# The order of high and low products in sixteen experts of a hybrid diffusion step

## The chip, the cores and the metric

The kernel runs on one core of a Trainium2 chip. The metric is device time in microseconds (us) of one execution. Lower is better. The engines are named as the profile names them: PE is TensorE (matmuls), PEld its weight loads, DVE is VectorE, ACT is ScalarE, POOL is GpSimd, SP is SyncE, which issues the loads of weights.

## The reference, cut to what matters

The program is one layer of a hybrid backbone: a token mixer, and then a mixture of experts in which every expert picks its own tokens. The change lies in the experts alone.

```python
# bsz 1; 16 experts; d 1024; f 2048; 128 latent tokens and 16 prompt tokens for each expert
hid = jax.nn.silu(jnp.einsum('becd,edf->becf', xs, w1)) * jnp.einsum('becd,edf->becf', xs, w3)
out = jnp.einsum('becf,efd->becd', hid, w2) * gate[..., None]
```

Weights and activations are fp32.

## The kernel before, in words

**Parts.** An fp32 weight chunk (`raw`, 512 rows by 512 columns, 1 MB) is split into a high part `hi` in fp32r (a cast on ACT, L1294) and a low part `lo` in bf16, which is the rest (a subtraction on DVE, L1300). The tokens `x2` hold their own high and low part side by side in 288 columns, `xb` the tokens in bf16 in 144 columns. A product needs both: a high matmul `hi` times 288 columns (L1485), and a low matmul `lo` times 144 columns (L1493), which adds to the second half of the same accumulator. `sums` then adds the two halves: a copy on ACT (L1498) and an add on DVE (L1499).

**An expert's first product** (w1 and w3). Four steps `fb`, in each the two weights `w`, and for each of these two chunks (the two halves of the 1024 rows) and two blocks `q` of 256 columns. A block is 16 high matmuls, then 16 low ones, then its `sums`. So an expert has 16 blocks.

**Its second product** (w2). Two halves `dh` of the output, in each four chunks `kq` and two accumulators `q`. For every chunk: 8 high and 8 low matmuls of `q` 0, 8 high and 8 low ones of `q` 1. `sums` stand behind the fourth chunk. The second half of the last expert is ordered in another way, two chunks at a time for each `q`.

**What sets the order.** The program is written out by hand: each engine runs its instructions in the order of the code, and waits on semaphores. `ahead(n)` issues the splits of the chunks before `n`, five chunks in front of the products (`AH` is 5), with the low part one chunk behind the high part:

```python
def sums(a, dst):
    b = ep.tile([P, 2, S], F32, name="bs", bufs=3)
    A.copy(b, a[:, :, S:2 * S])
    V.tensor_tensor(dst, a[:, :, :S], b, op=OP.add)
```

There are six buffers of `hi` and of `lo`, five of `raw`, and three accumulators `ac` (`acc_pair`, two PSUM banks each). When a low part is made, the load of the chunk five on is issued by SP (L1288).

**Small groups between the products.** Eight matmuls that make the next expert's list of tokens (`list_make`, L1168), eight transposes of its tokens (`to_cols`, L1424), and eight of the expert before for its result (`finish`, L1509) stand between two blocks. In the first expert a search for thresholds runs beside the products: `step` sends a group of eight small matmuls (L1394) behind a block's high matmuls, and each needs the `msk` (L1387) that DVE made of the one before. Its end leads to the list of the second expert and the gather of that expert's tokens (`xg`, L1335). In the last expert the half result is added into memory and read back (`last_half`, L1571) while the second half runs, and `last_add` (L1552) needs it.

Of the kernel before, what the change touches and what calls it, by code (L numbers as in the profile page):

```python
# [19 lines left out]
P = 128  # L20
# [16 lines left out]
KF = FF // P  # L37
CAP = 128
PCAP = 16
S = CAP + PCAP  # L40
# [9 lines left out]
def hybrid_step_kernel(ctx: ExitStack, tc: tile.TileContext, x_prompt, x_sample, state_lru, c, c_ctx,  # L50
# [4 lines left out]
    V, A, G, PE, SY = nc.vector, nc.scalar, nc.gpsimd, nc.tensor, nc.sync  # L55
# [179 lines left out]
    first = {"v": 512, "p": 0, "g1": 1536, "g2": 2560, "bp": 0, "bl": 0}  # L235
    need = []
    for i, (kind, j) in enumerate(seq):
        if kind == "m":
            q, h = divmod(j, 2)
            need.append((i, wm[h * 512:(h + 1) * 512, 2048 + q * 256:2048 + (q + 1) * 256], 4, 256))  # L240
        elif kind == "a":
            g, h = divmod(j, 4)
            need.append((i, wm[2 * h * P:2 * (h + 1) * P, :2 * D].rearrange("(k p) (z f) -> p k z f", p=P, z=2)
                         [:, :, :, g * 256:(g + 1) * 256], 2, 512))
        else:
            w = w_br_pool[0] if kind == "bp" else w_br_lru[0] if kind == "bl" else w_in[0]
            c0 = first[kind] + j * P
# [200 lines left out]
    for q in range(4):  # L448
        k = 2 * q
# [296 lines left out]
    while at[0] + 1 < len(seq):  # L746
        at[0] += 1
        i = at[0]
        kind, j = seq[i]
# [15 lines left out]
        w = spl.pop((kind, j))  # L765
        if kind == "bp":
            a3 = dense(w, KP, pool_sb["yh"], pool_sb["yl"], KP - 1 if j == 0 else 0)
        elif kind == "bl":
# [4 lines left out]
            for n, (y, ws) in enumerate(parts[::-1] if j == KD - 1 else parts):  # L773
                for ch in range(NCH):
                    cs = slice(ch * CH, (ch + 1) * CH)
                    for k in range(KD):
                        for w in ws:
                            PE.matmul(a3[:, ch, :CH], w[:, k, :], y[:, k, cs], start=n == 0 and k == 0 and w is hi,  # L778
                                      stop=n == 1 and k == KD - 1 and w is ws[-1])
# [73 lines left out]
    def row(r):  # L853
        return bass.AP(tensor=rows_d.tensor, offset=rows_d.offset + r * D, ap=[[0, P], [1, D]])
# [371 lines left out]
    n = 4  # L1226
    for i in [1, 0] + list(range(2, NT - 1)):
        n = max(n + 1, 2 * i + 2)
        a, b = (4, KD - 1)
# [52 lines left out]
    SKIP = ((0, 0, 0), (1, 0, 0), (2, 0, 0))  # L1282
    raw, hl, x3s = {}, {}, {}
# [41 lines left out]
    def ahead(n, lag=1):  # L1325
        while nxt[0] < min(n, NC + 1):
            split_hi(nxt[0])
            nxt[0] += 1
            while nxt[1] < nxt[0] - lag:
                split_lo(nxt[1])  # L1330
                nxt[1] += 1
# [143 lines left out]

    yps = {}

    def products(ws, x2, xb, first, last, step=None):


        for r in range(2):
            for a, w, c0, k0 in ws:
                for k in range(4):
                    kk = k0 + k
                    PE.matmul(a[:, r, :2 * S], w[0][:, k, c0 + r * P:c0 + (r + 1) * P], x2(kk), start=kk == first,  # L1485
                              stop=False)
            if step is not None:
                step(r)
        for r in range(2):
            for a, w, c0, k0 in ws:  # L1490
                for k in range(4):
                    kk = k0 + k
                    PE.matmul(a[:, r, S:2 * S], w[1][:, k, c0 + r * P:c0 + (r + 1) * P], xb(kk), start=False,  # L1493
                              stop=kk == last)

    def sums(a, dst):
        b = ep.tile([P, 2, S], F32, name="bs", bufs=3)
        A.copy(b, a[:, :, S:2 * S])  # L1498
        V.tensor_tensor(dst, a[:, :, :S], b, op=OP.add)  # L1499

    def acc_pair():
        return acc3.tile([P, 2, 512], F32, name="ac")
# [14 lines left out]
    last = {}  # L1517
# [87 lines left out]
    find = search()  # L1605
# [18 lines left out]
    base = 0  # L1624
    prev = None
    for e in range(E):
        x2, xb = X.pop(e)
        hh, hb = [], []
        if 0 < e < E - 1:
            hot = list_hot(ep, V, e + 1, slo[:, :, e + 1])  # L1630
        for fb in range(4):
            hs = []
            for w in range(2):
                h = ep.tile([P, 4, S], F32, name=f"h{w}")
                for q in range(2):
                    a = acc_pair()
                    products([(a, hl[base + i], q * 256, 4 * i) for i in range(2)], lambda k: x2[:, k, :],
                             lambda k: xb[:, k, :], 0, 7,
                             (lambda r: None if r == 0 else next(find, None)) if e == 0 and (fb, w, q) not in SKIP else None)
                    sums(a, h[:, 2 * q:2 * q + 2])  # L1640
                    if (e, fb, w, q) == (0, 3, 1, 0):
                        for _ in find:
                            pass
                        hot = list_hot(ep, V, 1, slo[:, :, 1])
                    if (w, q) != (1, 1):
                        ahead(base + q + 1 + AH)
                for i in range(2):
                    del hl[base + i]
                base += 2
                hs.append(h)  # L1650
                if w == 0:
                    A.activation(h, h, AF.Silu)
                if (e, fb, w) == (0, 0, 1):
                    A.dma_start(g2r, row(6))
                    prompt_gate()
                if fb == 1 and w == 0 and 0 < e < E - 1:
                    list_make(ep, e + 1, hot)
                    fetched = x_fetch(hn_d[:, :], lgi[:, e + 1:e + 2])
                if prev is not None and fb == 0 and w == 0:
                    finish(*prev)  # L1660
                    prev = None
                    if e == 8:
                        fp = finish_prompt(0)
                        next(fp)
                if e == 8 and (fb, w) in ((2, 0), (2, 1)):
                    next(fp, None)
                if e == 7 and (fb, w) == (2, 0):
                    pgr = x_fetch(hp_d[:, :], pgi[:, 1:2], "rows")
                if e == 7 and (fb, w) == (3, 1):
                    prompt_cols(1, pgr)  # L1670
            h1, h3 = hs
            hf = ep.tile([P, 4, 2 * S], F32R, name=f"hh{fb}")
            hg = ep.tile([P, 4, S], BF16, name=f"hb{fb}")
            ht = ep.tile([P, 4, S], F32, name="ht")
            V.tensor_tensor(ht, h1, h3, op=OP.mult)
            ahead(base + AH)
            A.copy(hf[:, :, :S], ht)
            A.copy(hg, ht)
            V.tensor_tensor(hf[:, :, S:], ht, hf[:, :, :S].bitcast(F32), op=OP.subtract)
            hh.append(hf)  # L1680
            hb.append(hg)
        ot = ep.tile([P, KD, S], F32, name="ot")
        if e % 8 == 0:
            yps[e // 8] = ep.tile([P, KD, P], F32, name="yps")
        quarter = None
        if e == E - 1:
            last_hot()
            A.activation(ready[:, 0:1], ready[:, 1:2], AF.Sqrt)
        hc, bc = lambda k: hh[k // 4][:, k % 4, :], lambda k: hb[k // 4][:, k % 4, :]
        aa = {}  # L1690
        for dh in range(2):
            for kq in range(4):
                n = 4 * dh + kq
                step = None if quarter is None else lambda r: next(quarter, None)
                if (e, dh) == (E - 1, 1):

                    q, i = divmod(kq, 2)
                    if i == 0:
                        aa[q] = acc_pair()
                    products([(aa[q], hl[base + j], q * 256, 4 * j) for j in (2 * i, 2 * i + 1)], hc, bc, 0, KF - 1, step)  # L1700
                    if i == 1:
                        sums(aa[q], ot[:, 4 + 2 * q:6 + 2 * q])
                else:
                    for q in range(2):
                        if kq == 0:
                            aa[q] = acc_pair()
                        products([(aa[q], hl[base + kq], q * 256, 4 * kq)], hc, bc, 0, KF - 1, step)
                        if kq == 3:
                            sums(aa[q], ot[:, 4 * dh + 2 * q:4 * dh + 2 * q + 2])
                ahead(base + kq + 1 + AH)  # L1710
                if (e, n) == (E - 1, 3):
                    last_half(ot)
                    fp = finish_prompt(1)
                    next(fp)
                    quarter = last_sums(ot)
                if (e, n) == (E - 1, 4):
                    x3s["fg"] = ew.tile([P, 8, 256], F32, name="raw", bufs=RB).rearrange("p a b -> p (a b)")[:, :D]
                    A.dma_start(x3s["fg"], bass.AP(tensor=final_g.tensor, offset=final_g.offset, ap=[[0, P], [1, D]]))
                if e == 0 and n == LM:
                    list_make(ep, 1, hot)  # L1720
                    fetched = x_fetch(hn_d[:, :], lgi[:, 1:2])
                if e + 1 < E and n == (XC if e == 0 else 1):
                    xf = x_cols(e + 1, fetched)
                if e + 1 < E and n == (XP if e == 0 else 3):
                    X[e + 1] = x_parts(xf)
            for i in range(4):
                del hl[base + i]
            base += 4
        q = (e % 8) * PCAP
        G.tensor_tensor(yps[e // 8][:, :, q:q + PCAP], ot[:, :, CAP:],  # L1730
                        modc[:, 2, 0, 8:, None].to_broadcast([P, KD, PCAP]), op=OP.mult)
        prev = (e, ot)
# [84 lines left out]
```

## Time and profile before

| | |
|---|---|
| median of 3 runs | 2134.88 us (2134.04 to 2135.07) |
| the profiled execution, its own time | 2133.28 us |
| its span (first to last instruction) | 2131.5 us |
| mean granted TensorE clock | 0.986 of full speed |
| busy share of the span: PE, PEld, DVE, ACT, POOL | 96%, 92%, 80%, 64%, 10% |
| experts' products | from about 812 us to the end |

The span and the profiled execution's own time belong together; the median is of other executions. A share of busy time is a mean over the program's stages. The granted clock is what the throttle gave to TensorE, as a share of full speed.

In the rows below, a row of a view by stage has the stretch (us from the span's start), its length, each engine's busy time with its count of instructions (PE, PEld, DVE, ACT, POOL), the granted clock, the mean busy share of the 16 DMA engines, and GB/s. A row in order of time has the start, the length, the engine, the line, the operation, what it writes from what, its shape and its count, and in brackets how long its engine sat idle before it and who ended that. Equal instructions that follow each other are one row. Matmuls are pipelined and their ends are modelled, so the time that a run of them takes is read from its start to the start of the next row. The names leave out numbers: `x` is `x2`, `ac` any accumulator. A row of waits has the total in us, how often, and the longest.

### The profile page before, as it was taken

What the parts mean: (1) busy time and instruction counts of PE and PEld (TensorE: products, weight loads), DVE (VectorE), ACT (ScalarE), POOL (GpSimd) and SP (SyncE); (2) the same over time, 40 slices, a digit from 0 to 9 for tenths busy, and PEclk for the clock granted to TensorE, in tenths of its full rate; (3) what the DMA queues carried; (4) which work ended last, traced back from release to release, by engine and by line L of the source; (5) the groups of instructions that cost most, each with busy time, mean ns of one, the idle gap of its engine ahead of it and who ended that gap; (6) DMA issues with size and microseconds to landing.
All of it is one profiled execution on the core that took longest, in us unless ns stands there. A gap on an engine that the chain in (4) does not pass through costs nothing.

```text
span 2131.5 us, 40527 instructions
## 1 busy us (share of the span) xinstructions
PE 2056.4 (96%) x17269; PEld 1962.2 (92%) x17269; DVE 1703.2 (80%) x1833; ACT 1359.8 (64%) x1442; POOL 208.9 (10%) x338
## 2 busy tenths in 40 slices
PE   7999999999999997899999999999999999999995
PEld 4899999999998876899999999999999999999994
DVE  7788987732336378988998998898998898898896
ACT  7577675321113236677877877777777777787783
POOL 0000001010102120010010010011011011001021
PEclk9999999999999999999999999999999999999997
DMA  8134434164654257799999999999999999999995
GB/s 268 58 117 130 128 96 130 56 220 118 205 169 164 109 178 280 278 320 329 343 334 329 336 339 325 342 346 322 329 341 327 334 344 327 334 337 333 334 312 183
DMA packets 304819, 543.91 MB, mean 255 GB/s; under 512 B 16299, under 2 KB 85627, under 8 KB 304638
## 3 DMA queue, kind: packets, MB, share of 16 engines
q1 hardware_dynamic: 285306, 478.56, 64.8%
q0 software_dynamic: 15728, 52.77, 8.5%
q10 hardware_dynamic: 3604, 9.98, 1.3%
q8 instruction: 135, 2.21, 0.4%
q14 instruction: 46, 0.38, 0.1%
HBM read 500.60 MB, written 40.67 MB: 254 GB/s over the span
## 4 chain that ended last, share of the span: by engine, by line
PE 88%; DVE 7%; ACT 2%; DMA 2%; issue 1%; SPq 0%; DVEq 0%; ACTq 0%; POOLq 0%
PE ac L1485 37%; PE ac L1493 17%; PE a L196 6%; PE a L197 6%; PE a L195 6%; PE a L778 5%; DVE lo L1300 2%; PE a L1004 2%; PE a L1006 2%; PE a L1005 2%; DMA xg<-hn_d,lgi 1%; PE tp L1042 1%; PE tp L667 1%; PE tp L1424 1%; PE tp L1509 1%
## 5 line engine op out<-in xcount | busy, mean ns | idle before, releaser
L1300 DVE TENSOR_TENSOR lo<-raw,hi 128x2048 bf16<-128x2048 f32 x384 | 871.2, 2282 | 0.0
L1294 ACT CAST hi<-raw 128x2048 fp32r<-128x2048 f32 x384 | 729.2, 1912 | 4.4 <-DMA raw<-in_exp_w_dram 2.4
L1485 PE MATMUL ac<-x,hi 128*128 128x288 f32 x4096 | 606.2, 300 | 0.0
L1485 PEld LDWEIGHTS ac<-x,hi 128*128 128x128 f32 x4096 | 553.0, 189 | 1.0 <-issue 0.9
L1493 PEld LDWEIGHTS <-lo 128*128 128x128 bf16 x6144 | 379.4, 98 | 36.1 <-DVE lo L1300 0.2
L1485 PE MATMUL ac<-hh,hi 128*128 128x288 f32 x2048 | 332.9, 304 | 0.0
L1498 ACT COPY bs<-ac 128x288 f32<-128x288 f32 x320 | 128.0, 400 | 288.0 <-PE ac L1493 287.7
L1493 PE MATMUL ac<-xb,lo 128*128 128x144 bf16 x4096 | 301.2, 227 | 0.0
L1485 PEld LDWEIGHTS ac<-hh,hi 128*128 128x128 f32 x2048 | 280.0, 189 | 0.0
L197 PE MATMUL a<-hn_hi,lo 128*128 128x384 f32 x624 | 209.8, 336 | 1.6 <-DVE lo L186 1.6
L195 PE MATMUL a<-hn_hi,hi 128*128 128x384 f32 x624 | 209.7, 336 | 0.0
L196 PE MATMUL a<-hn_lo,hi 128*128 128x384 f32 x624 | 209.6, 336 | 0.0
L1493 PE MATMUL ac<-hb,lo 128*128 128x144 bf16 x2048 | 171.8, 227 | 0.0
L1499 DVE TENSOR_TENSOR h<-ac,bs 128x288 f32<-128x288 f32 x256 | 116.0, 453 | 40.6 <-ACT bs L1498 40.2
L186 DVE TENSOR_TENSOR lo<-raw,hi 128x1024 fp32r<-128x1024 f32 (+1 forms) x77 | 88.3, 1165 | 64.4 <-ACT hi L185 64.4
L197 PEld LDWEIGHTS a<-hn_hi,lo 128*128 128x128 f32 x624 | 117.3, 188 | 2.0 <-DVE lo L186 2.0
L195 PEld LDWEIGHTS a<-hn_hi,hi 128*128 128x128 f32 x624 | 117.3, 188 | 0.4
L196 PEld LDWEIGHTS a<-hn_lo,hi 128*128 128x128 f32 x624 | 117.4, 188 | 0.0
L1730 POOL TENSOR_TENSOR yps<-ot,modc 128x128 f32<-128x128 f32 x16 | 36.0, 2247 | 734.6 <-DVE ot L1499 734.6
L185 ACT CAST hi<-raw 128x1024 fp32r<-128x1024 f32 (+1 forms) x77 | 75.9, 1003 | 45.7 <-PE a L196 36.2
L1499 DVE TENSOR_TENSOR ot<-ac,bs 128x288 f32<-128x288 f32 x64 | 29.3, 458 | 69.5 <-ACT bs L1498 69.5
L1335 POOL DMA_INDIRECT xg<-hn_d,lgi x16 | 45.0, 2813 | 258.4 <-ACT bs L1498 138.2
(443 smaller groups left out, 2602.5 us busy)
## 6 DMA issues: line engine op xcount, KB each, us to landing
raw<-in_exp_w_dram SPq DMA_DIRECT2D x380, 1024.0 KB, 7.2
raw<-in_w_in_dram SPq DMA_DIRECT2D x28, 512.0 KB, 4.7
raw<-in_w_mod_dram SPq DMA_DIRECT2D x28, 512.0 KB, 5.4
araw<-in_w_mod_dram SPq DMA_DIRECT2D x18, 256.0 KB, 4.4
g_d<-sg ACTq DMA_DIRECT2D x8, 576.0 KB, 3.2
yh_d<-yh POOLq DMA_DIRECT2D x8, 576.0 KB, 3.2
yl_d<-yl POOLq DMA_DIRECT2D x8, 576.0 KB, 4.6
m_d<-sg POOLq DMA_DIRECT2D x8, 576.0 KB, 4.2
```

The lines of the kernel that those rows point to most:

```text
L185: A.copy(h, raw)
L186: V.tensor_tensor(l, raw, h.bitcast(F32), op=OP.subtract)
L195: PE.matmul(out, whi, xhi, start=first, stop=False)
L196: PE.matmul(out, whi, xlo, start=False, stop=False)
L197: PE.matmul(out, wlo, xhi, start=False, stop=last)
L778: PE.matmul(a3[:, ch, :CH], w[:, k, :], y[:, k, cs], start=n == 0 and k == 0 and w is hi, stop=n == 1 and k == KD - 1 and w is ws[-1])
L1294: A.copy(hl[n][0], raw[n])
L1300: V.tensor_tensor(lo, r, hi.bitcast(F32), op=OP.subtract)
L1485: PE.matmul(a[:, r, :2 * S], w[0][:, k, c0 + r * P:c0 + (r + 1) * P], x2(kk), start=kk == first, stop=False)
L1493: PE.matmul(a[:, r, S:2 * S], w[1][:, k, c0 + r * P:c0 + (r + 1) * P], xb(kk), start=False, stop=kk == last)
L1498: A.copy(b, a[:, :, S:2 * S])
L1499: V.tensor_tensor(dst, a[:, :, :S], b, op=OP.add)
```

## The change

`products` is cut in two functions. `highs` sends the high matmuls of a block, or only its first one in each bank (`part` true), or all but these (`part` false); `lows` sends the low ones. In the first product the two blocks of a pair of chunks are sent as: all highs of block 0, the first highs of block 1 (they clear its accumulator), the lows of block 0, the lows of block 1, the other highs of block 1. The next pair starts with highs. The second product follows the table `PLAN` over its four chunks, where "H", "h" and "L" are highs, first highs, and lows. `sums` of a block stand where its last matmul is now sent, and the splits, loads and small groups stay at their places between the blocks.

```diff
-    def products(ws, x2, xb, first, last, step=None):
+    def highs(ws, x2, first, last, step=None, part=None):
         for r in range(2):
             for a, w, c0, k0 in ws:
                 for k in range(4):
                     kk = k0 + k
-                    PE.matmul(a[:, r, :2 * S], w[0][:, k, c0 + r * P:c0 + (r + 1) * P], x2(kk), start=kk == first,
-                              stop=False)
+                    if part is None or part == (kk == first):
+                        PE.matmul(a[:, r, :2 * S], w[0][:, k, c0 + r * P:c0 + (r + 1) * P], x2(kk), start=kk == first,
+                                  stop=kk == last)
             if step is not None:
                 step(r)
+
+    def lows(ws, xb, last):
         for r in range(2):
...
+    PLAN = (("H", 0), ("h", 1), ("L", 0), ("L", 1), ("H", 1)), (("H", 1), ("H", 0), ("L", 0), ("L", 1)), \
+        (("L", 1), ("L", 0), ("H", 0), ("H", 1)), (("H", 0), ("L", 0), ("L", 1), ("H", 1))
...
+                pairs = [None, None]
                 for q in range(2):
-                    a = acc_pair()
-                    products([(a, hl[base + i], q * 256, 4 * i) for i in range(2)], lambda k: x2[:, k, :],
-                             lambda k: xb[:, k, :], 0, 7,
-                             (lambda r: None if r == 0 else next(find, None)) if e == 0 and (fb, w, q) not in SKIP else None)
+                    step = (lambda r: None if r == 0 else next(find, None)) if e == 0 and (fb, w, q) not in SKIP else None
+                    for n in range(q, 2 - q):
+                        a = acc_pair()
+                        pairs[n] = [(a, hl[base + i], n * 256, 4 * i) for i in range(2)]
+                        highs(pairs[n], lambda k: x2[:, k, :], 0, None, None if n else step, True if n else None)
+                    lows(pairs[q], lambda k: xb[:, k, :], None if q else 7)
+                    if q:
+                        highs(pairs[q], lambda k: x2[:, k, :], 0, 7, step, False)
+                    a = pairs[q][0][0]
                     sums(a, h[:, 2 * q:2 * q + 2])
...
-                    products([(aa[q], hl[base + j], q * 256, 4 * j) for j in (2 * i, 2 * i + 1)], hc, bc, 0, KF - 1, step)
+                    ws = [(aa[q], hl[base + j], q * 256, 4 * j) for j in (2 * i, 2 * i + 1)]
+                    if i == 0:
+                        highs(ws, hc, 0, None, step)
+                        lows(ws, bc, None)
+                    else:
+                        lows(ws, bc, None)
+                        highs(ws, hc, None, KF - 1, step)
...
-                    for q in range(2):
-                        if kq == 0:
+                    left = [q for _, q in PLAN[kq]]
+                    for part, q in PLAN[kq]:
+                        left.remove(q)
+                        if kq == 0 and q not in aa:
                             aa[q] = acc_pair()
-                        products([(aa[q], hl[base + kq], q * 256, 4 * kq)], hc, bc, 0, KF - 1, step)
-                        if kq == 3:
-                            sums(aa[q], ot[:, 4 * dh + 2 * q:4 * dh + 2 * q + 2])
+                        end = KF - 1 if q not in left else None
+                        ws = [(aa[q], hl[base + kq], q * 256, 4 * kq)]
+                        if part == "L":
+                            lows(ws, bc, end)
+                        else:
+                            early = kq == 0 and q == 1
+                            highs(ws, hc, 0, end, None, (part == "h") if early else None)
+                        if end and kq == 3:
+                            sums(aa.pop(q), ot[:, 4 * dh + 2 * q:4 * dh + 2 * q + 2])
```

In the program as built, PE's order in a pair of blocks of the sixth expert's first product was this (`ac_12705` and `ac_12747` are the accumulators of blocks 0 and 1, `hi_12503` and `lo_12504` the parts of the pair's first chunk; rows that only go on with the same are left out):

```order
L1485 MATMUL ac_12705<-x2_12344,hi_12503 128x288 x4
L1485 MATMUL ac_12705<-x2_12344,hi_12549 128x288 x4
...
L1493 LDWEIGHTS lo_12504
L1493 MATMUL ac_12705<-xb_12345,lo_12504 128x144
...
L1485 MATMUL ac_12747<-x2_12344,hi_12503 128x288 x4
...
L1493 MATMUL ac_12747<-xb_12345,lo_12504 128x144
...
L1485 MATMUL ac_12807<-x2_12344,hi_12591 128x288 x4
```

At the same place PE's order is now this (block 1 has the accumulator `ac_12722`, and `ac_12807` is block 0 of the next pair):

```order
L1486 MATMUL ac_12705<-x2_12344,hi_12503 128x288 x4
...
L1486 MATMUL ac_12722<-x2_12344,hi_12503 128x288 x2
L1496 LDWEIGHTS lo_12504
L1496 MATMUL ac_12705<-xb_12345,lo_12504 128x144
...
L1496 MATMUL ac_12722<-xb_12345,lo_12504 128x144
...
L1486 MATMUL ac_12722<-x2_12344,hi_12503 128x288 x3
...
L1486 MATMUL ac_12807<-x2_12344,hi_12591 128x288 x4
```

The 32 lows of the two blocks follow each other, and so do the 14 other highs of block 1 and the 16 highs of the next block 0. Before, each block went from its highs to its lows.

In the same expert's second product PE's order was this at the second and third chunk (`hi_13113` and `hi_13155` are their high parts, L1424 the transposes of the next expert's tokens):

```order
L1485 MATMUL ac_13255<-hh1_12885,hi_13113 128x288 x8
...
L1493 MATMUL ac_13255<-hb1_12886,lo_13114 128x144
...
L1485 MATMUL ac_13272<-hh1_12885,hi_13113 128x288 x8
...
L1493 MATMUL ac_13272<-hb1_12886,lo_13114 128x144
...
L1424 MATMUL tp_13335<-ident_82,xg_12804 128x128 x4
L1424 MATMUL tp_13341<-ident_82,xg_12804 128x128 x4
L1485 MATMUL ac_13255<-hh2_13063,hi_13155 128x288 x8
```

PE's order there is now this (`ac_13264` is the accumulator of `q` 1):

```order
L1486 MATMUL ac_13264<-hh0_12691,hi_13067 128x288 x6
L1486 MATMUL ac_13264<-hh1_12885,hi_13116 128x288 x8
L1486 MATMUL ac_13255<-hh1_12885,hi_13116 128x288 x8
...
L1496 MATMUL ac_13255<-hb1_12886,lo_13117 128x144
...
L1496 MATMUL ac_13264<-hb1_12886,lo_13117 128x144
...
L1424 MATMUL tp_13335<-ident_82,xg_12804 128x128 x4
L1424 MATMUL tp_13341<-ident_82,xg_12804 128x128 x4
...
L1496 MATMUL ac_13264<-hb2_13064,lo_13156 128x144
```

The highs of the second chunk follow those of the first, and the third chunk starts with its lows, behind the transposes. On DVE, ACT, POOL and SP the instructions stand in the order that they had.

## Rows read from the trace of the kernel before

**Rows 1.** The page: busy time by engine.
```profile
PE 2056.4 (96%) x17269; PEld 1962.2 (92%) x17269; DVE 1703.2 (80%) x1833; ACT 1359.8 (64%) x1442; POOL 208.9 (10%) x338
```

**Rows 2.** The page: shares of the chain that ended last, by line.
```profile
PE ac L1485 37%; PE ac L1493 17%; PE a L196 6%; PE a L197 6%; PE a L195 6%; PE a L778 5%; DVE lo L1300 2%; PE a L1004 2%; PE a L1006 2%; PE a L1005 2%; DMA xg<-hn_d,lgi 1%; PE tp L1042 1%; PE tp L667 1%; PE tp L1424 1%; PE tp L1509 1%
```

**Rows 3.** Busy time by stage: first expert, a middle expert, the last half.
```profile
815.00:903.15 88.15, 75.11 (x833) 72.16 (x831) 85.19 (x109) 57.42 (x55) 4.08 (x2) 0.98 0.78 272
...
992.70:1071.40 78.70, 78.70 (x794) 76.39 (x793) 71.40 (x60) 61.06 (x61) 7.32 (x4) 1.00 0.96 335
...
2084.00:2104.00 20.00, 16.63 (x151) 15.06 (x150) 7.89 (x13) 3.78 (x13) 2.01 (x2) 1.00 0.72 235
```

**Rows 4.** Waits from 1000 to 1300 us: total us, times, longest us.
```profile
ACT bs L1498 <- PE ac L1493: 65.8, 64, 2.4
...
DVE ot L1499 <- ACT bs L1498: 15.3, 14, 1.5
DVE h L1499 <- ACT bs L1498: 10.6, 24, 0.5
```

**Rows 5.** PE in order of time: first product of a middle expert.
```profile
1018.90 2.36 PE L1485 MATMUL ac<-x,hi 128*128 128x288 f32 x16
1021.11 1.17 PE L1493 MATMUL ac<-xb,lo 128*128 128x144 bf16 x16
...
1037.98 2.23 PE L1485 MATMUL ac<-x,hi 128*128 128x288 f32 x15
```

**Rows 6.** PE in order of time: half a second product, next expert's start.
```profile
1294.18 1.31 PE L1485 MATMUL ac<-hh,hi 128*128 128x288 f32 x8
1295.34 0.68 PE L1493 MATMUL ac<-hb,lo 128*128 128x144 bf16 x8
...
1305.06 0.67 PE L1493 MATMUL ac<-hb,lo 128*128 128x144 bf16 x8
...
1307.15 2.10 PE L1485 MATMUL ac<-x,hi 128*128 128x288 f32 x14
```

**Rows 7.** PE in order of time: highs behind a small group.
```profile
1012.56 2.35 PE L1485 MATMUL ac<-x,hi 128*128 128x288 f32 x16
1014.75 0.42 PE L1493 MATMUL ac<-xb,lo 128*128 128x144 bf16 x4
```

**Rows 8.** Engines in order of time: sums of a second product.
```profile
1292.57 1.30 PE L1485 MATMUL ac<-hh,hi 128*128 128x288 f32 x8
1293.36 0.46 DVE L1499 TENSOR_TENSOR ot<-ac,bs 128x288 f32<-128x288 f32 x1 [1.52 <-ACT bs L1498]
1295.28 2.28 DVE L1300 TENSOR_TENSOR lo<-raw,hi 128x2048 bf16<-128x2048 f32 x1
```

**Rows 9.** First expert in order of time: search, a sum, transposes of gathered tokens.
```profile
861.10 0.55 PE L1394 MATMUL tp<-msk,ones 128*128 128x112 bf16 x8 [2.94 <-DVE msk L1387]
...
876.09 1.76 PE L1411 MATMUL tp<-gt,ones 128*128 128x16 bf16 x64
...
882.57 0.46 DVE L1499 TENSOR_TENSOR h<-ac,bs 128x288 f32<-128x288 f32 x1 [0.52 <-ACT bs L1498]
...
903.15 1.09 PE L1424 MATMUL tp<-ident,xg 128*128 128x128 f32 x8 [1.46 <-DMA xg<-hn_d,lgi]
```

**Rows 10.** Last expert in order of time: its last adds and last sum.
```profile
2101.02 0.40 ACT L1498 COPY bs<-ac 128x288 f32<-128x288 f32 x1 [1.82 <-PE ac L1493]
2101.36 0.69 DVE L1552 TENSOR_TENSOR raw<-raw,tp 128x512 f32<-128x512 f32 x1 [0.48 <-DMA raw<-x_d]
2101.97 0.45 DVE L1499 TENSOR_TENSOR ot<-ac,bs 128x288 f32<-128x288 f32 x1
```

**Rows 11.** Busy time by stage: behind that wait, and in heavy transfer.
```profile
861.40:866.00 4.60, 4.60 (x37) 4.60 (x34) 4.50 (x8) 2.88 (x3) 0.00 (x0) 0.63 0.67 223
...
1002.77:1004.98 2.21, 2.21 (x21) 2.14 (x18) 2.21 (x4) 1.92 (x2) 1.17 (x1) 1.00 1.04 398
```

**Rows 12.** Low weight loads from 1000 to 1300 us: busy us, mean ns, idle.
```profile
L1493 PEld LDWEIGHTS <-lo 128*128 128x128 bf16 x1464 | 90.2, 98 | 8.7
```

## The prediction

> **What bounds the kernel now.** I read the page first, then the chain, the stages, the waits, and PE in order of time. PE is busy for 96% of the span, DVE for 80% [rows 1], but means over stages decide nothing. In the chain the experts' highs (L1485) hold 37% and their lows (L1493) 17%; DVE's low parts hold 2% and the gather of tokens 1% [rows 2]. The stages say where each holds. In a middle expert (78.70 us) PE is busy all the time, DVE for 71.40, ACT for 61.06, at clock 1.00 [rows 3]; the list of waits there has ACT and DVE waiting for PE, and PE for nothing [rows 4]. So a middle expert is as long as PE's row of matmuls. The first expert is another matter: DVE is busy for 85.19 of 88.15 us and PE for 75.11 [rows 3], since the search hangs on DVE. So is the last half: PE is busy for 16.63 of 20 us [rows 3], and its last adds wait for data read back from memory [rows 10].
>
> **What a change of kind costs on PE.** In the first product a block is 16 highs and 16 lows. From 1018.90 to 1037.98 there are six of them, so 3.180 us each [rows 5]. In the second product it is 8 and 8; from 1294.18 to 1307.15 there are eight, so 1.621 each [rows 6]. Two of the second kind hold the same matmuls as one of the first, but go from lows to highs and back once more: 2 x 1.621 - 3.180 = 0.062 us for one such round trip. With the starts rounded to 0.01 us it lies between 0.058 and 0.067. Sixteen highs behind a small group take 1014.75 - 1012.56 = 2.19 us [rows 7], against 2.21 behind lows [rows 5]: highs that follow anything else pay the same, so a small group that comes to stand between highs makes a round trip too.
>
> **The change, part by part.**
>
> *Round trips in a middle expert.* Before: 16 in the first product, 16 in the second. After: one for each pair of chunks (8), three in each half of the second product (the table reads H, L, H, L, H, L, H, and the next half starts with H), so 14. Of the small groups, the results of the expert before and the list now stand between highs (2 more); the transposes stand between lows and cost nothing new. So 16 instead of 32. Experts 2 to 15 (fourteen) save 16 each, except that the eighth has one and the ninth two more small groups between highs: 224 - 3 = 221. **221 x 0.062 = 13.7 us.**
>
> *First expert.* DVE's row is full there and its order stays, so what PE gains is waited away. I take two things. First, the sum after the search's end: DVE sat idle for 0.52 us before it, since PE had a block's lows, the next block's highs and that block's lows to do behind the last search matmul [rows 9]. Now the first of these rows of lows is done elsewhere, 0.97 us (3.180 less the 2.21 from 1018.90 to 1021.11) [rows 5]. So that idle time goes, and with it the list, the gather and the transposes at 903.15, which waited for the gather [rows 9], come 0.5 earlier. Second, behind these transposes three round trips go: 0.2. **0.7 us.**
>
> *Last expert.* First product and first half: 24 round trips become 12. **0.7 us.** In its second half the last add waited until 2101.36 for data from memory, and the sum behind it on DVE started at 2101.97, though ACT's copy began at 2101.02 [rows 10]. That read starts from the first half's result, so PE's gain in this half (0.1 us or so) is worth nothing.
>
> *Two highs sent ahead* clear block 1's accumulator. They are the same instructions, earlier, and cost nothing by themselves.
>
> *What is needed earlier, and its cover.* The third chunk's lows now stand first in the chunk, ahead by its highs, 1.16 us [rows 6]. Low parts are early by far more: the one made from 1295.28 to 1297.56 [rows 8] is that of the half's last chunk, whose first lows start at 1305.06 [rows 6], 7.5 us later. If that cover were gone, up to 1.16 us in each half would stand on PE. An accumulator is also needed sooner. At a half's end the sum of `q` 0 is done at 1293.82, 1.25 us after its last low made way (1292.57) [rows 8]. Its buffer is taken again by the first high of `q` 1 in the next half. That stood 8 highs, 8 lows, 8 highs and 8 lows later (3.24 us), and now stands 8 lows, 8 highs and 8 highs later, 0.46 + 1.16 + 1.09 = 2.7 us (lows as 1.62 less 1.16; the second highs without the round trip). So the cover falls from 2.0 to 1.4 us, and DVE sat idle for 1.52 us before that sum [rows 8], so nothing holds it up. In the first product the distance from block 0's sum to the next use falls by about 1.4 us too, to 5 us, which is long.
>
> *DVE and the loads* have the same work in an expert that gets 1 us shorter: DVE 71.4 of 77.7 us. The loads go from 335 GB/s [rows 3] to 339; a stretch with more of them shows 398 [rows 11].
>
> Sum: 13.7 + 0.7 + 0.7 = 15.1. The profiled execution took 2133.28 us (2131.5 and 1.8 around it), so it would take 2118.2. The median of the runs lies 1.6 above it, and from there I forecast 2134.88 - 15.1 = **2119.8 us**. About 0.2% (4.3 us) is what a measurement of this kernel can tell from no change.
>
> **The rivals.**
>
> *Changes of kind are free.* Then 3.180 against 2 x 1.621 has another cause, such as the number of times that PE turns to another accumulator or chunk, which the change leaves nearly as it is. The time stays at 2134.9. Against it: the 2.19 us behind a small group [rows 7] has no such turn that other runs lack. The Trainium skill (TensorE: Matmul & The Clock Gate, "Part 2: What happens when you issue a matmul") has the next weights load while the present matmul runs, so that matmuls follow each other at the length of their columns. By that rule the order of kinds would not matter and the sum would be 0; the trace shows 0.062 us that it does not explain. The same end comes if the loads already set the pace: the DMA engines' busy share is 0.96 [rows 3]. Against that, ACT's casts, which need the loads, are not in the list of waits [rows 4], and 398 GB/s were moved at a share of 1.04 [rows 11]. Together 0.06.
>
> *Long rows of lows don't hold their pace* (slower). A low weight load takes 98 ns [rows 12], while lows follow each other at about 61 ns (0.97 us for 16), so loads overlap by reserve. No row of before has more than 16 lows. If the reserve were used up behind the sixteenth, each further low would cost up to 37 ns. A middle expert has about 150 of these (128 in the first product, 16 or more in the second), so 5.5 us each, 83 in 15 experts: 2119.8 + 83 = 2203. The gain is gone at 1.0 us / 150 = 6.6 ns each, and the kernel is slower by over 0.2% from 8.5. Against it: 64 small matmuls behind each other, each with a weight load of its own, took 1.62 us to the next row, 25 ns each [rows 9], with no sign of a reserve that runs out. 0.05.
>
> *The first expert gets longer.* PE runs further ahead of the search there, and waits longer in one piece. After the longest wait now (2.94 us [rows 9]) the granted clock was 0.63 in the next 4.6 us [rows 11], which is 3.4 us at 1.2 GHz and the rest at 2.4. The search's small groups also stand unevenly now, two close together and then a long way apart. If in three of the four steps `fb` half speed makes a group late by up to 1.7 us (half of these 3.4 us), and nothing on DVE takes it up, 5 us come back: 2124.9. For it: DVE is full. Against it: PE has 13 us of idle time in that expert [rows 3]. 0.10.
>
> *A sum comes too late for its accumulator.* If a whole low part (2.28 us) came in front of the sum, 0.9 us over the cover would be lost in each expert, 13 in all: 2133. Against it stands DVE's idle time before it [rows 8]. 0.04.
>
> **How the numbers follow.** The forecast and its near neighbours have 0.75. Their own range: with 0.058 to 0.067 for a round trip the sum goes from 14.2 to 16.3, and with 0 to 1.5 us for the first expert from 13.5 to 17.1, so 2117.8 to 2121.4. The range to hold 8 in 10 takes in the first expert's loss above, and a little below for a price that I read too low: 2116 to 2125.5. Faster by over 0.2% (under 2130.6) are the forecast, the first expert's loss and half of the late sums: 0.87. Within 0.2%: free changes, loads that set the pace and the rest of late sums: 0.08. Slower: 0.05.
>
> **What would show it.** In the profile after, a middle expert takes 77.7 us instead of 78.7, and a pair of blocks 6.30 instead of 6.36. PE's list of waits there stays empty. DVE's idle time before the first sum of a half stays near 1 us or more. Rows of 32 lows take 32 x 0.061 = 1.95 us. The transposes of the first expert come at 902.6, and the end comes some 15 us earlier with the last half as long as it was. I am wrong if a middle expert takes 78.5 or more, if PE waits for a sum or a low part, or if the first expert ends later than before.

## The result, and the profile after

The median went from 2134.46 us (four runs, 2131.6 to 2135.07) to 2117.47 (three runs, 2115.17 to 2117.47): a ratio of 0.9919, with a 95% interval of 0.99 to 0.9939. A fourth run of the change took 7123.09 us, which no run here explains, and is in none of these numbers. The profiled execution took 2117.47 us, with a span of 2115.7: 15.8 less than before, where the sum of the forecast said 15.1.

The page after has one line each for the engines' busy time and for the chain by line. In the code after, L1486 are the highs, L1496 the lows, L1506 and L1507 the copy and the add of `sums`.

```profile
PE 2043.0 (97%) x17269; PEld 1967.8 (93%) x17269; DVE 1703.8 (81%) x1833; ACT 1363.9 (64%) x1442; POOL 199.2 (9%) x338
```

```profile
PE ac L1486 37%; PE ac L1496 17%; PE a L196 6%; PE a L197 6%; PE a L195 6%; PE a L778 5%; DVE lo L1300 2%; PE a L1004 2%; PE a L1006 2%; PE a L1005 2%; DMA xg<-hn_d,lgi 1%; PE tp L667 1%; PE tp L1424 1%; PE tp L1042 1%; PE tp L1517 1%
```

The counts, and the chain's shares by line, are those of [rows 1, 2]. PE's busy time is 13.4 us less for the same 17269 matmuls: the gain lies in PE's own row. The stages show it (the first row spans most of the first expert, the second is a middle expert):

```profile
812.00:902.00 90.00, 79.52 (x851) 76.68 (x851) 88.17 (x111) 60.13 (x58) 4.08 (x2) 0.95 0.79 275
991.50:1069.20 77.70, 77.70 (x794) 76.61 (x794) 71.42 (x61) 61.30 (x61) 6.52 (x5) 1.00 0.98 342
```

The same 794 matmuls fill 77.70 us instead of 78.70 [rows 3], at the same clock of 1.00. PE in order of time, in a first product; the last row is the list of tokens three experts on:

```profile
1001.00 4.47 PE L1486 MATMUL ac<-x,hi 128*128 128x288 f32 x32
1005.31 2.17 PE L1496 MATMUL ac<-xb,lo 128*128 128x144 bf16 x32
1007.29 2.09 PE L1486 MATMUL ac<-x,hi 128*128 128x288 f32 x14
1009.22 0.36 PE L1168 MATMUL tp<-parts,hot 128*128 128x5 bf16 x8
1009.45 2.62 PE L1486 MATMUL ac<-x,hi 128*128 128x288 f32 x18
1011.91 2.17 PE L1496 MATMUL ac<-xb,lo 128*128 128x144 bf16 x32
1013.89 4.47 PE L1486 MATMUL ac<-x,hi 128*128 128x288 f32 x32
1018.21 1.99 PE L1496 MATMUL ac<-xb,lo 128*128 128x144 bf16 x29
...
1242.30 0.35 PE L1168 MATMUL tp<-parts,hot 128*128 128x5 bf16 x8
```

A pair of blocks takes 1018.21 - 1011.91 = 6.30 us (6.36 before), and 32 lows 1.98. From list to list is the length of an expert: (1242.30 - 1009.22) / 3 = 77.69. Before it was 78.68 (the lists started at 1012.35 and 1248.39). The waits from 1000 to 1300 us (total, times, longest):

```profile
ACT bs L1506 <- PE ac L1496: 32.0, 27, 2.2
...
ACT bs L1506 <- PE ac L1486: 29.9, 38, 1.2
DVE ot L1507 <- ACT bs L1506: 13.4, 15, 1.3
DVE h L1507 <- ACT bs L1506: 8.9, 32, 0.4
```

PE is not among those who wait, as in [rows 4]. ACT now waits for highs in 38 cases, since blocks now end on highs too.

### The profile page after: what moved, and what is told of

The parts are those of the page before. It is cut to its first block, busy times and chain, and to the rows that moved or that the text cites. A ratio compares the mean times of both kernels' runs of the same rounds, so it can differ in the third digit from the quotient of the medians.

```text
span 2115.7 us, 40527 instructions
## 1 busy us (share of the span) xinstructions
PE 2043.0 (97%) x17269; PEld 1967.8 (93%) x17269; DVE 1703.8 (81%) x1833; ACT 1363.9 (64%) x1442; POOL 199.2 (9%) x338
## 4 chain that ended last, share of the span: by engine, by line
PE 88%; DVE 7%; ACT 2%; DMA 2%; issue 1%; SPq 0%; DVEq 0%; ACTq 0%; POOLq 0%
PE ac L1486 37%; PE ac L1496 17%; PE a L196 6%; PE a L197 6%; PE a L195 6%; PE a L778 5%; DVE lo L1300 2%; PE a L1004 2%; PE a L1006 2%; PE a L1005 2%; DMA xg<-hn_d,lgi 1%; PE tp L667 1%; PE tp L1424 1%; PE tp L1042 1%; PE tp L1517 1%
## 5 line engine op out<-in xcount | busy, mean ns | idle before, releaser
L1486 PE MATMUL ac<-x,hi 128*128 128x288 f32 x4096 | 586.7, 298 | 0.0
L1486 PEld LDWEIGHTS ac<-x,hi 128*128 128x128 f32 x4096 | 549.3, 188 | 1.0 <-issue 0.9
L1496 PEld LDWEIGHTS <-lo 128*128 128x128 bf16 x6144 | 385.0, 98 | 16.3
L1486 PE MATMUL ac<-hh,hi 128*128 128x288 f32 x2048 | 297.7, 298 | 0.0
L1506 ACT COPY bs<-ac 128x288 f32<-128x288 f32 x320 | 127.9, 400 | 261.4 <-PE ac L1486 130.4
L1496 PE MATMUL ac<-xb,lo 128*128 128x144 bf16 x4096 | 280.7, 227 | 0.0
L1486 PEld LDWEIGHTS ac<-hh,hi 128*128 128x128 f32 x2048 | 275.5, 188 | 0.0
L1496 PE MATMUL ac<-hb,lo 128*128 128x144 bf16 x2048 | 146.8, 226 | 0.0
L1507 DVE TENSOR_TENSOR h<-ac,bs 128x288 f32<-128x288 f32 x256 | 115.7, 452 | 33.2 <-ACT bs L1506 32.7
L1507 DVE TENSOR_TENSOR ot<-ac,bs 128x288 f32<-128x288 f32 x64 | 29.3, 458 | 60.3 <-ACT bs L1506 60.3
L701 ACT ACTIVATE sg<-a 128x1152 f32<-128x1152 f32 x16 | 18.2, 1135 | 79.3 <-PE a L197 79.2
```

## The experiments

Ratios are against the kernel before on the same chip, whose median was 2134.0 to 2134.5 us each time. "Expert" is the distance from list to list in a middle expert, "trips" the round trips low to high to low counted in its program.

| kernel | trips | expert, us | time, us | ratio (95%) |
|---|---|---|---|---|
| before | 32 | 78.68 | 2134.46 | 1 |
| the change | 16 | 77.69 | 2117.47 | 0.9919 (0.99 to 0.9939) |
| e1, first product alone | 26 | 78.29 | 2126.89 | 0.9967 (0.9953 to 0.9981) |
| e2, second product alone | 22 | 78.10 | 2125.55 | 0.9957 (0.9941 to 0.9974) |
| e3, trips doubled | 64 | 80.67 | 2162.86 | 1.0136 (1.0119 to 1.0153) |
| e4, turns of accumulator | 16 | 77.69 | 2120.0 | 0.9932 (0.9915 to 0.9949) |
| e5, long lows, old order | 32 | 100.16 | 2461.04 | one run |
| e6, long lows, new order | 16 | 100.01 | 2457.65 | one run |
| e7, fewest trips | 12 | 77.45 | 2116.21 | 0.9918 (0.9904 to 0.9932) |
| e8, the change again | 16 | 77.69 | 2117.48 | 0.9921 (0.9907 to 0.9934) |
| e9, fewest, transposes later | 12 | 77.45 | 2111.88 | 0.9894 (0.9879 to 0.9909) |
| e10, the change, transposes later | 16 | 77.69 | 2116.39 | 0.9918 (0.9904 to 0.9931) |

**e1 and e2: each half of the change alone.** In e1 the second product is sent as before; in e2 the first is.

```diff
...
 e1, from the change, second product
+                        ws = [(aa[q], hl[base + kq], q * 256, 4 * kq)]
+                        highs(ws, hc, 0, None, step)
+                        lows(ws, bc, KF - 1)
...
 e2, from the change, first product
+                    ws = [(a, hl[base + i], q * 256, 4 * i) for i in range(2)]
+                    highs(ws, lambda k: x2[:, k, :], 0, None, step)
+                    lows(ws, lambda k: xb[:, k, :], 7)
...
```

> The new order in the first product alone; the second product goes from highs to lows as before. Theory (a round trip from lows to highs and back costs 0.062 us): a middle expert has 26 of them, 6 fewer than before, so 78.3 us where before has 78.7 and the change 77.7. With 15 experts and about 1 us in the first one that is 6 to 7 us: about 2128. Rival (what costs is the turn to another accumulator or chunk): about as many turns as before, 2134.

> The new order in the second product alone; the first product as before. Theory: 22 round trips in a middle expert, 10 fewer, so 78.1 us; 9.3 us in 15 experts, and little in the first expert: about 2125. Rival (turns): no change, 2134.

The lists in PE's order of time, three experts apart, in e1 and then in e2:

```profile
1009.95 0.36 PE L1168 MATMUL tp<-parts,hot 128*128 128x5 bf16 x8
...
1244.82 0.35 PE L1168 MATMUL tp<-parts,hot 128*128 128x5 bf16 x8
```

```profile
1014.20 0.35 PE L1168 MATMUL tp<-parts,hot 128*128 128x5 bf16 x8
...
1248.50 0.34 PE L1168 MATMUL tp<-parts,hot 128*128 128x5 bf16 x8
```

e1 takes 0.39 us from an expert for 6 trips, e2 0.58 for 10: 0.065 and 0.058 for each, and 0.97 together where the change takes 0.99. The two parts add up.

In the first expert e1 gives nothing (101.17 us from its first high to the next expert's, 101.22 before). DVE in order of time says why:

```profile
867.14 0.28 DVE L1395 SCALAR_TENSOR_TENSOR met<-tp,cand 128x112 f32<-128x112 f32 x1 [0.63 <-PE tp L1394]
```

and, by stage, the stretch before:

```profile
859.30:864.40 5.10, 5.10 (x43) 4.95 (x42) 5.00 (x9) 2.31 (x3) 0.00 (x0) 0.50 0.75 238
```

PE had sat idle for 3.90 us and then got a clock of 0.50, that is 1.2 GHz throughout. A group of the search came late by 0.63, and DVE waited. The first product has the same order in the change, and PE waited 3.90 us there too; what differs is the clock behind the wait, 0.62 there.

**e3: trips doubled.** The order of before, but with the lows of each bank (`r`) directly behind its highs, so 8 highs and 8 lows, and 4 and 4 in the second product.

```diff
             if step is not None:
                 step(r)
-        for r in range(2):
             for a, w, c0, k0 in ws:
                 for k in range(4):
                     kk = k0 + k
                     PE.matmul(a[:, r, S:2 * S], w[1][:, k, c0 + r * P:c0 + (r + 1) * P], xb(kk), start=False,
```

> The kernel before, with the lows of each of a block's two banks sent right behind the highs of that bank. Round trips double to 64 in a middle expert, while turns from bank to bank become fewer (two in a block instead of four). Theory: 32 x 0.062 = 2.0 us more in a middle expert, 80.7, and 28 to 31 in all: about 2164. Rival (turns): the same time or less, 2134 or below.

The two lists in PE's order of time:

```profile
1012.91 0.35 PE L1168 MATMUL tp<-parts,hot 128*128 128x5 bf16 x8
...
1254.93 0.34 PE L1168 MATMUL tp<-parts,hot 128*128 128x5 bf16 x8
```

They give 242.02 / 3 = 80.67: 1.99 us for 32 more trips, 0.062 each. The kernel is slower by 1.36%, with the same matmuls and chunks.

**e4: turns of accumulator.** The change, with the 32 lows of a pair sent in turn to block 0 and block 1.

```diff
-                    lows(pairs[q], lambda k: xb[:, k, :], None if q else 7)
+                    if q == 0:
+                        for r in range(2):
+                            for i in range(2):
+                                for k in range(4):
+                                    for n in range(2):
+                                        a, wt, c0, k0 = pairs[n][i]
+                                        PE.matmul(a[:, r, S:2 * S], wt[1][:, k, c0 + r * P:c0 + (r + 1) * P],
+                                                  xb[:, k0 + k, :], start=False, stop=n == 0 and k0 + k == 7)
```

> The changed kernel, with the 32 lows of a pair of blocks in the first product sent in turns, one of block 0, one of block 1: 31 turns from accumulator to accumulator in a row instead of a few, the same round trips. Theory: a middle expert stays at 77.7 us, all at 2117. Rival (turns, a round trip's 0.062 us being two of them): some 28 more turns in each of 8 pairs, 224 x 0.031 = 7 us more in an expert, over 2200.

An expert stays at 77.69 us, though PE now turns to another accumulator at each of these lows: that costs nothing that these runs show. The total is 2.5 us above the change's. Its first expert is 1.2 us longer (100.73 against 99.50; the sum of block 0 there waits 0.95 us, since its last low now stands at the end of the 32), and its experts start 2.3 us later in the profiled run, in a stage that it does not touch.

**e5 and e6: long lows.** In the order of before (e5) and in that of the change (e6), the lows have 288 columns, the 144 of `xb` twice; so the low part is counted twice in the result.

```diff
-                    PE.matmul(a[:, r, S:2 * S], w[1][:, k, c0 + r * P:c0 + (r + 1) * P], xb(kk), start=False,
-                              stop=kk == last)
+                    PE.matmul(a[:, r, :2 * S].rearrange("p (z s) -> p z s", z=2), w[1][:, k, c0 + r * P:c0 + (r + 1) * P],
+                              xb(kk)[:, None, :].to_broadcast([P, 2, S]), start=False, stop=kk == last)
```

> The kernel before with lows of 288 columns instead of 144: each reads its 144 columns twice and adds them to both halves of the accumulator, so the low part is counted twice in the result. To be read against the same lows in the changed order, next run. Lows then follow each other at about 0.122 us, so a middle expert takes some 23 us more, about 101. Theory A (a round trip costs because the first high's weight load does not fit behind a low of 0.06 us): with long lows the load is hidden, the round trip costs under 0.015 us, and both orders take the same to within 0.25 us an expert. Theory B (a fixed price for each change of kind): the orders stay 1.0 us an expert apart.

> The changed kernel with the same lows of 288 columns (the low part counted twice in the result). Theory A: a middle expert within 0.25 us of the run before, both about 101 us. Theory B: 1.0 us shorter than the run before.

PE in order of time in e5 (a list, a last low, the highs behind it, the same highs from the second on, a list) and then in e6:

```profile
1045.81 0.35 PE L1168 MATMUL tp<-parts,hot 128*128 128x5 bf16 x8
...
1050.06 0.29 PE L1493 MATMUL ac<-xb,lo 128*128 128x288 bf16 x1
1050.09 0.78 PE L1485 MATMUL ac<-x,hi 128*128 128x288 f32 x4
...
1050.31 0.56 PE L1485 MATMUL ac<-x,hi 128*128 128x288 f32 x3
...
1246.13 0.34 PE L1168 MATMUL tp<-parts,hot 128*128 128x5 bf16 x8
```

```profile
1045.26 0.36 PE L1168 MATMUL tp<-parts,hot 128*128 128x5 bf16 x8
...
1245.28 0.35 PE L1168 MATMUL tp<-parts,hot 128*128 128x5 bf16 x8
```

Two experts lie between these lists: 100.16 and 100.01 us each (other experts of e5 without an extra small group take up to 100.22). So with long lows 16 trips cost 0.15 to 0.21 us, 0.01 each, where they cost 0.99 with short ones. The price of a trip is not fixed; most of it goes when the low is long. A long low also writes both halves of the accumulator, as a high does, and no run takes its length and this apart. The same place in the change, with short lows:

```profile
1007.26 0.23 PE L1496 MATMUL ac<-xb,lo 128*128 128x144 bf16 x1
1007.29 0.77 PE L1486 MATMUL ac<-x,hi 128*128 128x288 f32 x4
...
1007.50 0.56 PE L1486 MATMUL ac<-x,hi 128*128 128x288 f32 x3
```

From the start of the last low to that of the second high it is 0.24 us here and 0.25 in e5. The step of a low is 0.063 or 0.123 us (the median from start to start in the traces), that of a high 0.132. Long lows want 0.123 + 0.132 = 0.255 for these two steps, so nothing is lost; short ones want 0.195, and about 0.05 is lost. That is about three quarters of the price. The rest, about 0.01, is what a trip still costs with long lows.

**e7: fewest trips.** The change with another table, two trips in each half; the list and the result moved to between lows, and from the second expert on the transposes one chunk earlier.

```diff
-    PLAN = (("H", 0), ("h", 1), ("L", 0), ("L", 1), ("H", 1)), (("H", 1), ("H", 0), ("L", 0), ("L", 1)), \
-        (("L", 1), ("L", 0), ("H", 0), ("H", 1)), (("H", 0), ("L", 0), ("L", 1), ("H", 1))
+    PLAN = (("H", 0), ("H", 1), ("L", 0), ("L", 1)), (("L", 1), ("L", 0), ("H", 0), ("H", 1)), \
+        (("H", 1), ("H", 0), ("L", 0), ("L", 1)), (("L", 1), ("L", 0), ("H", 0), ("H", 1))
...
-                if e + 1 < E and n == (XC if e == 0 else 1):
+                if e + 1 < E and n == (XC if e == 0 else 0):
                     xf = x_cols(e + 1, fetched)
```

> The changed kernel with still fewer round trips: the second product's four chunks go highs, lows; lows, highs; highs, lows; lows, highs (two round trips in a half instead of three), and the three small groups stand between lows. A middle expert has 12 round trips, 4 fewer than the change: 0.25 us less, 77.44 us, 3.7 us in all, about 2113.5. Rival (a sum too late for its accumulator): the sums of a half now both stand at its end, and the accumulator of the second block is wanted 2.1 us behind the last high of the first, 0.9 us after its sum is done; if that cover fails, PE waits up to 1 us twice in an expert, and the time is 2117 to 2140.

> The changed kernel itself, timed beside the run before it on one chip: 2115 to 2118 if its first measurement stands; a middle expert 77.7 us.

The lists in PE's order of time in e7:

```profile
1015.03 0.35 PE L1168 MATMUL tp<-parts,hot 128*128 128x5 bf16 x8
...
1247.38 0.34 PE L1168 MATMUL tp<-parts,hot 128*128 128x5 bf16 x8
```

An expert is 0.24 us shorter for four trips, and PE waits for nothing from 930 to 2050 us: accumulators used again sooner do no harm. But the time, forecast at 2113.5 us, cannot be told from that of e8, the change run beside it. PE in order of time in the first expert:

```profile
902.40 1.80 PE L1424 MATMUL tp<-ident,xg 128*128 128x128 f32 x8 [2.46 <-DMA xg<-hn_d,lgi]
904.00 2.13 PE L1496 MATMUL ac<-hb,lo 128*128 128x144 bf16 x16
905.87 4.55 PE L1486 MATMUL ac<-hh,hi 128*128 128x288 f32 x32
```

and the stretch behind the wait, by stage:

```profile
902.40:905.90 3.50, 3.50 (x25) 3.44 (x25) 2.01 (x1) 2.25 (x3) 0.00 (x0) 0.53 1.05 388
```

PE waits 2.46 us for the gathered tokens, 1.17 more than in the change (1.29 at 901.37), and then goes on at a clock of 0.53. That PE comes earlier is the smaller part of the 1.17: counted from the first high, it comes to the transposes 0.16 us sooner, the gather is issued 0.06 later, and it takes 9.65 us instead of 8.70. The first expert takes 102.14 us.

**e9 and e10: the first expert's transposes one chunk later**, in e7 and in the change.

```diff
-    LM, XC, XP = 0, 4, 5
+    LM, XC, XP = 0, 5, 5
```

> The kernel with the fewest round trips, whose first expert took 2.6 us longer than the changed kernel's: PE came to the transposes of the second expert's tokens earlier, waited 2.5 us for their gather, and then ran them and the next lows at half pace. Here these transposes stand one chunk later, behind the second chunk of the second half. If the wait for the gather made the loss, PE finds the tokens there, the first expert gets 3 to 4 us shorter (102.1 to about 98.4), the middle experts stay at 77.45, and all takes about 2112.5, ratio about 0.990. Rival (the first expert is long for another reason, a sum that comes late in the new order): it stays near 102, and all at 2116.

> The changed kernel with the same transposes one chunk later and nothing else. If the wait for the gather (1.3 us at these transposes) is what the first expert still loses, it takes 98.2 us instead of 99.5, and all takes about 2116; the middle experts stay at 77.7. Rival: no change.

PE in order of time in e9:

```profile
902.17 2.37 PE L1486 MATMUL ac<-hh,hi 128*128 128x288 f32 x16
904.38 1.03 PE L1424 MATMUL tp<-ident,xg 128*128 128x128 f32 x8
905.16 2.36 PE L1486 MATMUL ac<-hh,hi 128*128 128x288 f32 x16
```

No wait stands before the transposes. They take 0.78 us to the next row, and 16 lows take 0.97 [rows 5]; in e7 both together took 905.87 - 902.40 = 3.47. So 2.46 of wait and 1.7 of half clock are gone, 4.2 us. The first expert takes 97.81 us, 4.33 less. The median falls by 4.33 too, to 2111.88, but on another chip, and the profiled executions differ by 3.0 only, since in e9 the experts start 1.4 us later. This is the fastest kernel here: its slowest run (2113.19) is faster than the fastest of e10, which ran on the same chip (2114.95), though their intervals overlap by 0.0005. In the change itself (e10) the step takes 1.5 us from the first expert (98.01 instead of 99.50), but the times cannot tell it from none: 2116.39 against 2117.48.

## Why the prediction held, step by step

**The price of a trip, 0.062 us.** Right, and shown to be the cause: from 12 trips to 64 an expert goes from 77.45 to 80.67 us, 0.062 for each of 52, and e1, e2 and the change lie on this line within 0.03 us. The prediction gave no reason for the price. e5 and e6 give its condition: it is there when the low ahead of a change is short. A possible reason is the weight load of the first high. The page after has it, in its groups of instructions:

```profile
L1486 PEld LDWEIGHTS ac<-x,hi 128*128 128x128 f32 x4096 | 549.3, 188 | 1.0 <-issue 0.9
L1496 PEld LDWEIGHTS <-lo 128*128 128x128 bf16 x6144 | 385.0, 98 | 16.3
```

It takes 188 ns, against 98 for a low's, and one step of a low covers only 63 of them. That it is the load and not another part of a high's start was argued, not shown: no run changed the load alone. Nor do the lengths alone give the price: 188 ns are more than the step of a long low (123) or of a high (132) as well, and behind these nothing is lost.

The Trainium skill (TensorE: Matmul & The Clock Gate, "Part 2: What happens when you issue a matmul") has the next weights load while the present matmul runs. Read with e5 and e6, that overlap leaves almost nothing to pay behind long lows, 0.01 us for a trip, and does not hide all of it behind short ones, 0.062. That matmuls would then follow each other at the length of their columns, whatever their kind, was the prediction's own step, and the trips contradict it. The same page's section on LDWEIGHTS sets a load by its columns alone, 128 / 1.2 = 107 ns as an estimate for both kinds; the trace has 188 and 98, so the measurement decides, and in these rows the two kinds differ.

**Middle experts, 13.7 us.** Right. Experts 2 to 15 took 13.84 less in the profiled run. The eighth gained 0.94 (79.52 to 78.58), as its one extra small group said, and the ninth 0.93 (80.44 to 79.51), where two such groups should have left 0.87.

**First expert, 0.7 us.** Mis-sized: 1.72 (101.22 to 99.50). Rows of it, on PE and DVE:

```profile
860.84 0.55 PE L1394 MATMUL tp<-msk,ones 128*128 128x112 bf16 x8 [3.90 <-DVE msk L1387]
...
861.55 3.81 PE L1496 MATMUL ac<-xb,lo 128*128 128x144 bf16 x32
865.17 2.09 PE L1486 MATMUL ac<-x,hi 128*128 128x288 f32 x14
...
881.60 0.46 DVE L1507 TENSOR_TENSOR h<-ac,bs 128x288 f32<-128x288 f32 x1
...
901.37 1.09 PE L1424 MATMUL tp<-ident,xg 128*128 128x128 f32 x8 [1.29 <-DMA xg<-hn_d,lgi]
```

The experts' first high started at 812.50 us before and at 812.28 after. Counted from there, the sum behind the search came 0.75 sooner (70.07 to 69.32; forecast 0.5) with no idle time before it, and the gather was issued 0.76 sooner. The gather then took 8.70 us instead of 9.50, which was not forecast, and the trips behind the transposes gave some 0.2. So the transposes came at 901.37, not at 902.6 as forecast: the order of events was right, and two sizes were not. Both owe something to luck. The earlier sum hangs on the clock: of the six profiles whose first product has this order (the change, e1, e7 to e10) five issue the gather 0.70 to 0.76 sooner than before, and e1, with its clock of 0.50, not at all. The gather's length stays open: it was 8.5 to 8.7 in the change, e4, e8 and e10, and 9.4 to 9.7 in the six others with short lows. No run took apart what else the DMA engines carried then.

**Last expert, 0.7 us.** It gave nothing (113.57 to 113.55 us, to the end). Its first product and first half gave 0.8. Its second half was to stay as long as it was, and took 0.8 more: the read back from memory, in the chain after,

```profile
2076.76 8.35 DMA raw<-x_d
```

took 8.35 us instead of 7.87, and another 0.3 came behind it. From the second pair of the first half's transposes (L1562, after L1570) to the end it was 47.67 us before and 48.47 in the change. The eight other profiles with short lows gave 47.4 to 48.1, and e8, the same kernel, 47.5, so no part of the change is behind it that these runs could show.

**The cover.** Right. On DVE the first sum of a half still has idle time ahead of it:

```profile
1286.73 0.46 DVE L1507 TENSOR_TENSOR ot<-ac,bs 128x288 f32<-128x288 f32 x1 [1.26 <-ACT bs L1506]
```

1.26 us instead of 1.52 [rows 8], "near 1 us or more" as said. With less cover still (e7) nothing waits.

**The rivals.** *Changes of kind are free*: fallen by e3, which has the same matmuls, turns from bank to bank less often, and is 28.8 us longer. Turns of accumulator cost nothing that shows (e4). Loads set no pace: 342 GB/s went through in the shorter expert (335 in [rows 3]). *Long rows of lows don't hold their pace*: fallen, 32 lows took 1.98 us: 0.97 for the first 16 [rows 5] and 1.01, 0.063 each, for the next. Over the forecast's 1.95 that is 0.03, and the pair of blocks came out at its 6.30 all the same. *The first expert gets longer*: its mechanism is real, its size was not 5 us. PE's longest wait grew from 2.94 [rows 9] to 3.90, and the 32 lows from 861.55 took 3.62 us instead of 1.98, at a granted clock of 0.62 from 860.84 to 865.30. In the change DVE took that up. In e1 it did not, by 0.63 us, and the first term of the first expert was gone. *A sum comes too late*: fallen by e7.

**The sum.** The span fell by 15.8 us: the experts start 0.2 sooner, the first one gives 1.7, experts 2 to 15 give 13.8 and the last one nothing. That this lies within 0.7 of the forecast 15.1 is in part luck, since the first expert gave 1.0 more than its term and the last one 0.7 less. The median fell by 17.0, to 2117.47, inside the range of 2116 to 2125.5 but just under the forecast's own 2117.8 to 2121.4; the runs of one kernel differ by more than that. The ratio's interval reaches from 13.0 to 21.3 us, so it is the profile, not the medians, that tells the terms apart.

## What to carry to other kernels

Where matmuls with large and small weight loads alternate, count the changes from the small to the large kind and read the price of one from two rows of different length; group by kind as far as accumulators and operands allow. A price that goes when the matmul ahead is longer suggests that this matmul was too short for something behind it; what that is needs a run of its own. When PE gets faster, look next at what it waits for: here the gather of the second expert's tokens, whose longer wait and the half clock behind it took back 2.6 of the 3.4 us that e7 gained in experts 2 to 15, until the transposes moved by one chunk.

## What was not expected of the hardware

- The same round trip costs 0.062 us where a low has a step of 0.063, and 0.01 where it has one of 0.123.
- 32 lows, each with weights of its own, to two accumulators in turn at each matmul, run as fast as in two rows of 16 (e4).
- A wait of 2.46 us on PE cost another 1.7 behind it, at a clock of 0.53 (e7). After the 1.29 us wait at the same place in the change the clock stayed at 1.00. The length of a wait alone does not say which: behind 2.52 us of it in the kernel before the clock was 1.00 (842.90 to 846.00 us), behind 2.48 us in the change 0.67 (824.59 to 829.00).
- A middle expert's length is the same to 0.01 us in the change, e4, e8 and e10, while the first expert, which hangs on DVE, a gather and the clock, varied from 97.8 to 102.1 us among kernels that gave PE much the same work there.
